# Splitting the first store of a row softmax into a 16-partition DMA and a 112-partition DMA

## The chip, the cores and the metric

The kernel runs on one core of a Trainium2 chip. A core has several engines that run at once: TensorE (unused here), VectorE (DVE in the profile), ScalarE (ACT), GpSimd (POOL) and SyncE (SP). Data moves between the chip's main memory (HBM) and the on-chip memory of 128 partitions (SBUF) by DMA; sixteen DMA engines do the moving, whichever engine issues the transfer. The metric is the device time of one execution in microseconds (us), as the median of several runs. A profiled execution also has a span, from its first to its last instruction in the trace, which is a little shorter than its own time.

## The reference

The input has 16 x 1024 rows of 512 float32 values, 33.55 MB. Each row becomes a softmax with temperature 0.5:

```python
def reference(x: np.ndarray) -> np.ndarray:
    temp = 0.5
    x_scaled = x / temp
    x_max = np.max(x_scaled, axis=-1, keepdims=True)
    exp_x = np.exp(x_scaled - x_max)
    return (exp_x / np.sum(exp_x, axis=-1, keepdims=True)).astype(np.float32)
```

The output has the same size, so 67.1 MB have to cross between HBM and SBUF.

## The kernel before, in words

The 16,384 rows are cut into eight chunks of 4 MB. In a chunk each of the 128 partitions holds 16 consecutive rows (G = 16), which is one unbroken piece of 32 KB in HBM. Six buffers hold chunks (BUFS = 6); chunks 6 and 7 go into the buffers of chunks 0 and 1 and can be loaded only when those have been stored.

SyncE issues the loads (`load`, L68): chunk 0 in two DMAs, the others in one each. Of chunk 7 the last row of each partition is loaded by GpSimd (`load_last_row`, L97), after it has copied one finished sum (L90) so that it starts late. The first six chunks are issued without waiting for any buffer.

Compute goes block by block; a block is a chunk or, in chunks 0 and 7, a part of one (BLOCKS; eleven blocks in all, three of them in chunk 0). For each block VectorE takes the negated row maxima (`shift`, L77) and doubles them (L81). ScalarE computes exp(2x + bias) row by row in place, summing each row as it goes (`exponentials`, L108). VectorE inverts the sums (L125) and multiplies most rows by them (`scale_vector`, L127), and ScalarE does the remaining rows (`scale_scalar`, L138). When the last block of a chunk is scaled, ScalarE issues the chunk's store, a DMA of 4 MB (`store`, L148). So the store instruction stands in ScalarE's own stream, between exponentials.

The order on each engine is written out by hand in the loop at the end of the kernel: the exponentials of block i+1 go ahead of the scaling of block i, the maxima of block i+2 follow, then the store of block i. Blocks 0, 1 and 2 are chunk 0, so the first store comes in the round of block 2; two exponentials of block 3 (chunk 1) are held back in that round and stand right behind the store (`rows`, with its cut of 2 for chunk 1).

`finished` collects the names of all loads, of all stores but the last chunk's, and of a few last instructions; a no-operation on SyncE at the end depends on them all. The DMA queues are named q1 (loads from SyncE), q10 (stores from ScalarE) and q0 (the two loads from GpSimd) in the profile.

Of the kernel before, what the change touches and what calls it, by code (L numbers as in the profile page):

```python
# [1 line left out]

# [4 lines left out]


@with_exitstack
def kernel(  # L10
    ctx: ExitStack,
    tc: tile.TileContext,
    x: bass.AP,
    out: bass.AP,
):
    nc = tc.nc
    fp32 = mybir.dt.float32
    P = nc.NUM_PARTITIONS
    AX = mybir.AxisListType.X
    EXP = mybir.ActivationFunctionType.Exp  # L20
    COPY = mybir.ActivationFunctionType.Copy
    MAX = mybir.AluOpType.max

    D = x.shape[-1]
    xf = x.flatten_outer_dims()
    of = out.flatten_outer_dims()
    N = xf.shape[0]

    G = 16
    C = N // (P * G)
    assert C * P * G == N
    xr = xf.rearrange("(c p g) d -> c p g d", p=P, g=G)
    outr = of.rearrange("(c p g) d -> c p g d", p=P, g=G)
    WHOLE = [(0, G)]
    LOADS = [[(0, 4), (4, G)]] + [WHOLE] * 6 + [[(0, G - 1)]]
    BLOCKS = [[(0, 4), (4, 8), (8, G)]] + [WHOLE] * 6 + [[(0, 8), (8, G)]]
    STORES = [WHOLE] * 8  # L40
    BMAX = 16
    BUFS = 6

    data = ctx.enter_context(tc.tile_pool(name="data", bufs=BUFS))
    stats = ctx.enter_context(tc.tile_pool(name="stats", bufs=6))

    ctx.enter_context(tc.manual_schedule())


    warm = stats.tile([P, 1], fp32, name="warm", bufs=1)  # L50
    nc.vector.memset(warm, 0.0)  # L51
    nc.scalar.activation(out=warm, in_=warm, func=EXP)  # L52

    chunks = {}
    blocks = [(c, lo, hi) for c in range(C) for lo, hi in BLOCKS[c]]
    n = len(blocks)
    biases, sums, recips = {}, {}, {}

    finished = []

    def load(c):
        if c < BUFS:
            chunks[c] = data.tile([P, G, D], fp32, name="xt")
        else:
            chunks[c] = chunks[c - BUFS]
        xt = chunks[c]
        for lo, hi in LOADS[c]:
            part = nc.sync.dma_start(out=xt[:, lo:hi, :], in_=xr[c][:, lo:hi, :])  # L68
            finished.append(part.ins.name)

    def shift(i):
        c, lo, hi = blocks[i]
        if c not in chunks:
            load(c)
        b = hi - lo
        negmax = stats.tile([P, BMAX], fp32, name="negmax")
        nc.vector.tensor_reduce(  # L77
            negmax[:, 0:b], chunks[c][:, lo:hi, :], axis=AX, op=MAX, negate=True
        )
        biases[i] = stats.tile([P, BMAX], fp32, name="bias")  # L80
        nc.vector.tensor_scalar_mul(biases[i][:, 0:b], negmax[:, 0:b], 2.0)  # L81

    def load_last_row(signal):
        seen = stats.tile([P, 1], fp32, name="seen", bufs=1)
        copied = nc.gpsimd.tensor_copy(out=seen, in_=signal)  # L90
        finished.append(copied.ins.name)
        c = C - 1
        halves = "p (h d) -> p h d"
        to = chunks[c - BUFS][:, G - 1, :].rearrange(halves, h=2)
        of_ = xr[c][:, G - 1, :].rearrange(halves, h=2)
        for p0, p1 in ((P - 2, P), (0, P - 2)):
            part = nc.gpsimd.dma_start(  # L97
                out=to[p0:p1], in_=of_[p0:p1], max_dma_last_dim=2 * D
            )
            finished.append(part.ins.name)  # L100

    def exponentials(i, rows):
        c, lo, hi = blocks[i]
        if i not in sums:
            sums[i] = stats.tile([P, BMAX], fp32, name="sums")
        for g in rows:
            row = chunks[c][:, lo + g, :]
            nc.scalar.activation(  # L108
                out=row,
                in_=row,  # L110
                func=EXP,
                bias=biases[i][:, g : g + 1],
                scale=2.0,
                accum_out=sums[i][:, g : g + 1],
            )
            if c == BUFS - 1 and g == 10:
                load_last_row(sums[i][:, g : g + 1])


    def scale_vector(i):  # L120
        c, lo, hi = blocks[i]
        b = hi - lo
        k = b - b // 8
        recips[i] = stats.tile([P, BMAX], fp32, name="recip")
        nc.vector.reciprocal(recips[i][:, 0:b], sums[i][:, 0:b])  # L125
        rows = chunks[c][:, lo : lo + k, :]
        last = nc.vector.tensor_mul(  # L127
            rows, rows, recips[i][:, 0:k].unsqueeze(2).broadcast_to((P, k, D))
        )
        if i == n - 1:  # L130
            finished.append(last.ins.name)

    def scale_scalar(i):
        c, lo, hi = blocks[i]
        b = hi - lo
        for g in range(b - b // 8, b):
            row = chunks[c][:, lo + g, :]
            last = nc.scalar.activation(  # L138
                out=row, in_=row, func=COPY, scale=recips[i][:, g : g + 1]
            )  # L140
            if i == n - 1:
                finished.append(last.ins.name)

    def store(i):
        c, _, end = blocks[i]
        for lo, hi in STORES[c]:
            if hi == end:
                part = nc.scalar.dma_start(  # L148
                    out=outr[c][:, lo:hi, :], in_=chunks[c][:, lo:hi, :]
                )  # L150
                if c < C - 1:
                    finished.append(part.ins.name)

    shift(0)
    shift(1)

    def rows(i):
        c, lo, hi = blocks[i]
        cut = hi - lo - (2 if c == 1 else 0)
        return range(cut), range(cut, hi - lo)  # L160

    exponentials(0, rows(0)[0])
    for i in range(n):
        if i + 1 < n:
            exponentials(i + 1, rows(i + 1)[0])
        scale_vector(i)
        scale_scalar(i)
        if i + 2 < n:
            shift(i + 2)
        store(i)  # L170
        if i + 1 < n:
            exponentials(i + 1, rows(i + 1)[1])

    seen = nc.sync.nop()
    info = mybir.DependencyInfo(
        mybir.DependencyClass.Sync, mybir.DependencyReason.DATA
    )
    for name in finished:
        tc.add_manual_dep(seen.ins, name, info, reason="leaves one wait for the end")


# [1 line left out]
_INS = ['x']  # L183
_OUTS = [((16, 1024, 512), 'float32')]


# [23 lines left out]
```

## Time and profile before

| what | value |
|---|---|
| median of three runs | 161.78 us (161.74 to 161.98) |
| the profiled execution's own time | 162.29 us |
| its span | 160.5 us |
| VectorE busy | 134.6 us, 84% |
| ScalarE busy | 102.2 us, 64% |
| GpSimd busy | 1.9 us, 1% |
| bytes moved by DMA | 67.13 MB, mean 418 GB/s over the span |
| a store (4 MB), issue to landing | 23.1 us in the median |
| a full load (4 MB), issue to landing | 34.8 us in the median |

Busy time is the sum of an engine's instructions; issuing a DMA is not counted in it. "Issue to landing" counts from the issuing instruction to the completion, so it includes time in which the transfer stood in the queue behind others or shared the DMA engines with them. In the profile's row of slices the span is cut into 40 equal parts, a digit being the busy share in tenths, and a row below gives the GB/s moved in each slice. L numbers are lines of the kernel.

### The profile page before, as it was taken

The page shows a single profiled execution, that of the slowest core. Times are in us where ns is not written, and L with a number is a line of the kernel's source. Part 1 is how long each engine was busy: PE and PEld are TensorE (multiplying, and loading weights), DVE is VectorE, ACT ScalarE, POOL GpSimd, SP SyncE. Part 2 cuts the span into 40 slices and gives each one's busy share as a digit, 9 for nine tenths or more (in the row PEclk, how much of TensorE's full clock was granted, in tenths as well). Part 3 has the DMA queues.
Part 4 walks back from the last instruction along what each step waited for, and adds up shares of the span by engine and source line. Part 5 has one row for each costly group of instructions (what it writes and reads, how often), then busy time and mean ns, then how long its engine had stood idle before and what let it go on. Part 6 is the DMA issues. An engine that isn't in the chain of part 4 may idle for free.

```text
span 160.5 us, 411 instructions
## 1 busy us (share of the span) xinstructions
DVE 134.6 (84%) x45; ACT 102.2 (64%) x273; POOL 1.9 (1%) x7
## 2 busy tenths in 40 slices
DVE  0607999999999999999999999999999999957000
ACT  3071549069989963998199909991899891790000
POOL 0000000000000000000000000030000000000000
DMA  5999999999989999999999999989999999999994
GB/s 184 470 408 498 400 392 457 457 392 402 506 269 425 490 392 400 506 400 392 490 425 392 474 434 392 490 383 483 422 450 400 400 465 441 392 457 449 400 441 204
DMA packets 2578, 67.13 MB, mean 418 GB/s; under 512 B 328, under 2 KB 328, under 8 KB 400
## 3 DMA queue, kind: packets, MB, share of 16 engines
q1 hardware_dynamic: 1296, 33.29, 49.3%
q10 hardware_dynamic: 1152, 33.55, 48.4%
q0 software_dynamic: 128, 0.26, 0.4%
q14 instruction: 2, 0.02, 0.0%
HBM read 33.55 MB, written 33.55 MB: 418 GB/s over the span
## 4 chain that ended last, share of the span: by engine, by line
DVE 75%; DMA 7%; issue 5%; ACT 3%; SPq 0%
DVE negmax L77 42%; DVE xt L127 31%; DMA xt<-in_x_dram 7%; ACT xt L108 3%; DVE bias L81 1%; DVE recip L125 1%; SPq L68 0%
## 5 line engine op out<-in xcount | busy, mean ns | idle before, releaser
L108 ACT ACTIVATE xt<-xt,bias 128x512 f32<-128x512 f32 x128 | 90.4, 708 | 41.5 <-DVE bias L81 40.6
L77 DVE TENSOR_REDUCE negmax<-xt 128x16 f32<-128x8192 f32 (+2 forms) x11 | 69.9, 6352 | 9.4 <-DMA xt<-in_x_dram 9.4
L127 DVE TENSOR_TENSOR xt<-xt,recip 128x7168 f32<-128x7168 f32 (+2 forms) x11 | 62.0, 5637 | 0.4
L108 ACT ACTIVATION_READ_ACCUMULATOR xt<-xt,bias 128x1 f32 x128 | 23.9, 187 | 0.0
L138 ACT ACTIVATE xt<-xt,recip 128x512 f32<-128x512 f32 x15 | 9.9, 706 | 0.0
L125 DVE RECIPROCAL recip<-sums 128x16 f32<-128x16 f32 (+2 forms) x11 | 2.4, 218 | 1.8 <-ACT xt L108 1.8
L81 DVE TENSOR_SCALAR bias<-negmax 128x16 f32<-128x16 f32 (+2 forms) x11 | 1.9, 173 | 0.4
L52 ACT ACT_TABLE_LOAD x1 | 1.3, 1283 | 0.7 <-PEq L194 0.7
L97 POOL DMA_DIRECT2D xt<-in_x_dram x2 | 1.5, 741 | 0.5 <-issue 0.5
L90 POOL COPY seen<-sums 128x1 f32<-128x1 f32 x1 | 0.2, 184 | 103.6 <-ACT xt L108 103.6
L51 DVE MEMSET warm<- 128x1 f32 x1 | 0.1, 59 | 0.8 <-PEq L194 0.8
L52 ACT ACTIVATE warm<-warm 128x1 f32<-128x1 f32 x1 | 0.2, 202 | 0.0
L194 POOL MEMSET const-float32-0.0<- 128x1 f32 x1 | 0.1, 93 | 0.2 <-issue 0.2
L194 POOL MEMSET const-bfloat16-1.0<- 128x1 bf16 x1 | 0.1, 95 | 0.0
L194 POOL MEMSET const-uint8-127<- 128x1 uint8 x1 | 0.1, 95 | 0.0
L194 POOL MEMSET const-float32-1.0<- 128x1 f32 x1 | 0.1, 93 | 0.0
## 6 DMA issues: line engine op xcount, KB each, us to landing
out_dram<-xt ACTq DMA_DIRECT2D x8, 4096.0 KB, 23.1
xt<-in_x_dram SPq DMA_DIRECT2D x6, 4096.0 KB, 34.8
xt<-in_x_dram SPq DMA_DIRECT2D x1, 3840.0 KB, 27.8
xt<-in_x_dram SPq DMA_DIRECT2D x1, 3072.0 KB, 11.6
xt<-in_x_dram SPq DMA_DIRECT2D x1, 1024.0 KB, 4.8
xt<-in_x_dram POOLq DMA_DIRECT2D x1, 252.0 KB, 15.4
xt<-in_x_dram POOLq DMA_DIRECT2D x1, 4.0 KB, 9.1
```

The lines of the kernel that those rows point to most:

```text
L51: nc.vector.memset(warm, 0.0)
L52: nc.scalar.activation(out=warm, in_=warm, func=EXP)
L77: nc.vector.tensor_reduce(negmax[:, 0:b], chunks[c][:, lo:hi, :], axis=AX, op=MAX, negate=True)
L81: nc.vector.tensor_scalar_mul(biases[i][:, 0:b], negmax[:, 0:b], 2.0)
L90: copied = nc.gpsimd.tensor_copy(out=seen, in_=signal)
L97: part = nc.gpsimd.dma_start(out=to[p0:p1], in_=of_[p0:p1], max_dma_last_dim=2 * D)
L108: nc.scalar.activation(out=row, in_=row, func=EXP, bias=biases[i][:, g : g + 1], scale=2.0, accum_out=sums[i][:, g : g + 1],)
L125: nc.vector.reciprocal(recips[i][:, 0:b], sums[i][:, 0:b])
L127: last = nc.vector.tensor_mul(rows, rows, recips[i][:, 0:k].unsqueeze(2).broadcast_to((P, k, D)))
L138: last = nc.scalar.activation(out=row, in_=row, func=COPY, scale=recips[i][:, g : g + 1])
L194: nc = _bacc.Bacc("TRN2", target_bir_lowering=False, num_devices=1)
```

## The change

The store of chunk 0 becomes two DMAs from the same instruction stream, one after the other: the first stores partitions 0 to 15, the second partitions 16 to 127. Sixteen partitions are sixteen pieces of 32 KB; the other DMA has 112 pieces. The stores of chunks 1 to 7 stay single DMAs of 128 partitions. Both new DMAs enter the list `finished`, and the load of chunk 6, which takes chunk 0's buffer, depends on both. The order of all other instructions on every engine is the same as before; ScalarE's stream has one instruction more.

```diff
     STORES = [WHOLE] * 8
+
+    SPLIT = [(0, 16), (16, P)]
     BMAX = 16
...
         for lo, hi in STORES[c]:
             if hi == end:
-                part = nc.scalar.dma_start(
-                    out=outr[c][:, lo:hi, :], in_=chunks[c][:, lo:hi, :]
-                )
-                if c < C - 1:
-                    finished.append(part.ins.name)
+                for p, q in SPLIT if c == 0 else [(0, P)]:
+                    part = nc.scalar.dma_start(
+                        out=outr[c][p:q, lo:hi, :], in_=chunks[c][p:q, lo:hi, :]
+                    )
+                    if c < C - 1:
+                        finished.append(part.ins.name)
```

## The prediction

> **What bounds the kernel now.** I read the slices first, to see which resource is full from end to end, then the DMA queues, to turn that into a sum, then the waits and the timeline around the first store and the last.
>
> ```profile
> DVE  0607999999999999999999999999999999957000
> ACT  3071549069989963998199909991899891790000
> ...
> DMA  5999999999989999999999999989999999999994
> GB/s 184 470 408 498 400 392 457 457 392 402 506 269 425 490 392 400 506 400 392 490 425 392 474 434 392 490 383 483 422 450 400 400 465 441 392 457 449 400 441 204
> ```
>
> The DMA engines are full from the first slice to the last, also after VectorE and ScalarE have stopped. One slice of about 4 us falls out: 44 to 48 us at 269 GB/s, where the first store is issued.
>
> ```profile
> q1 hardware_dynamic: 1296, 33.29, 49.3%
> q10 hardware_dynamic: 1152, 33.55, 48.4%
> q0 software_dynamic: 128, 0.26, 0.4%
> ```
>
> Loads are q1, stores q10, the last row's loads q0; together 98.1% of 16 engines. The 1152 packets of q10 are eight stores of 128 pieces (one partition, 32 KB) and 16 completions. 48.4% of 160.5 us is 77.7 us per engine for 64 pieces: 1.21 us a piece, 27 GB/s per engine. No compute stage can be shortened to any use here; a microsecond in which an engine moves nothing is a microsecond at the end.
>
> ```profile
> SPq L68 <- DMA out_dram<-xt: 74.7, 2, 55.8
> DVE negmax L77 <- DMA xt<-in_x_dram: 9.4, 2, 4.8
> 43.36 0.71 ACT L138 ACTIVATE xt<-xt,recip 128x512 f32<-128x512 f32 x1
> 44.10 0.37 ACTq L148 DMA_DIRECT2D out_dram<-xt  x1
> 44.52 0.72 ACT L108 ACTIVATE xt<-xt,bias 128x512 f32<-128x512 f32 x1 [0.45 <-ACT xt L138]
> 46.31 0.72 ACT L108 ACTIVATE xt<-xt,bias 128x512 f32<-128x512 f32 x1 [0.27 <-DVE bias L81]
> 147.48 0.34 ACTq L148 DMA_DIRECT2D out_dram<-xt  x1
> ```
>
> The first two are waits (total, times, longest), the rest the timeline: VectorE waits for loads only at the start (twice), SyncE's two last loads wait for stores 0 and 1, and the first and last stores go out at 44.10 and 147.48 us. The chain of waits names VectorE for 75% of the span, but it ends with the last multiply at 147.4 us and leaves out the store behind it: it is not what sets the end.
>
> The trace's records of single DMA packets give the sum (their clock stands about 10.1 us ahead of the span). The first data packet starts at 2.0 us, the last ends at 159.45, and 1.05 us follow. At the usual duration of each size the packets of an engine make 155.55 us; they took 157.49, so 1.93 us are stretched packets: 0.53 in the first 2 us, 0.3 scattered, and **1.08 us per engine in 18 load packets between 45 and 49 us**, which took 1.36 to 2.49 us in place of 1.21. They begin before any store packet moves (the first at 48.66 us). No such stretch stands where later stores, or later loads, are queued behind running ones. So the first store costs about 1.1 us at its start, once.
>
> [...] from 50 us on store and load packets of 1.21 us alternate. [...]
>
> **The change part by part.** It removes one issue of a 4 MB store and adds two, of 0.5 and 3.5 MB; bytes and pieces are the same, the other seven stores are untouched.
>
> *ScalarE's queue.* One more issue of 0.34 to 0.37 us at 44.5 us. Behind it stand two exponentials of block 3 (44.52 and 45.24) and block 4's. ScalarE was idle for 0.27 us at 46.31, so block 4 starts about 0.1 us late; the next gap, 4.0 us before 62.93, swallows that, and VectorE wants these sums only at 62.80, when the last was done at 57.7. Without that cover it would cost 0.37 us. Cost: 0.
>
> *Completions.* q10 gets 16 more packets (1168), one of 9 ns per engine: 0.01 us. Since that packet takes one turn of the store queue, the loads move one piece ahead: no byte more.
>
> *Waits.* Load 6 waits for two DMAs in place of one. Store 0 lands at 68.5 us by the packets, the load queue has work until 75.3 to 76.8: at least 6.8 us of cover. The closing wait gets one more name that is long done: 0.
>
> *The start of the first store (1.08 us today).* Not resolved by the trace. If it is a fixed price of waking the store queue, nothing changes: 0. If it lasts while the descriptors of that DMA are written, a first DMA with an eighth of them pays an eighth: 1.08 x 7/8 = 0.94 us gained, 1.08 at most. I take 0 here, since the stretch was about one piece long (1.21 us) and one piece each is still what comes first.
>
> *The 16-partition piece.* Sixteen engines each read 32 KB from partitions 0 to 15. [...] In the trace three engines took their first store piece about 1.2 us before the other thirteen, so their reads would be almost over; [...] **2.7 us**. I take this.
>
> *The 112-partition piece.* [...] Load turns fall between them[...], so I take 0 in the forecast and 2.1 at the upper end.
>
> Sum: 0 + 0.01 + 0 + 0 + 2.7 = +2.7 us on a saturated stream, 1:1 at the end. The profiled execution took 162.29 us with a span of 160.5, so 1.8 us lie outside, unchanged; its new span would be 163.2. It stands 0.5 us above the median of the runs, 161.78; I put the difference on the median: **164.5 us**.
>
> **The rivals.**
>
> *The wake-up stretch shrinks[...]: faster.* For it: the dip is the one clear hole in the stream, at just this store, and stores queued behind a running one show none. Against it: that a shorter first DMA shortens it rests on the descriptor reading alone. Time: 161.78 - 0.94 = 160.85. [...] There is room at the end: the last store is issued at 147.5 us and the engines finish the one before between 148.7 and 149.8, so 1.2 us can be gained before compute limits.
>
> *Nothing moves.* The stretch is a fixed price, and [...] waiting engines move loads. Time: 161.8.
>
> [...] 2.7 + 2.1: 166.6. [...]
>
> **How the numbers follow.** A measurement of this kernel tells about 0.2% (0.32 us) from nothing. Contention: 0.50, of which 0.15 at 0.4 to 1.5 us (reads partly hidden), 0.22 around 2.7, 0.13 from 3.5 to 4.8. Faster: 0.29, between 160.7 and 161.4. Nothing: 0.21. So the time is that of the middle contention case, 164.5; the range from 160.8 to 166.0 leaves out the very end on both sides, about 0.05 below and 0.07 above. The likeliest case alone is 162.3 to 166.6.
>
> **What would show it.** Right: q10 at 1168 packets with a share of 50% or more in place of 48.4%; store packets of partitions 0 to 15 of 2 to 5 us just after 48 us; a slice of 48 to 52 us well below 400 GB/s; the first store landing 2 to 3 us later, the multiplies and exponentials at the same durations, and the last packet near 162 us. If all 32 KB store packets stay at 1.21 us, [...] the sum of the load stretch near 46 to 49 us tells whether the change gains (near 0.1 us left) or does nothing (1.1 us again). A stretch that grows with the second DMA, or a load queue running dry before load 6, would be a loss that I have not counted.

## The result and the profile after

The changed kernel takes 167.53 us in the median of six runs (165.31 to 167.74), against 161.78 us before: 5.75 us more, a ratio of 1.0321 with a 95% interval of 1.0265 to 1.0377. The direction was forecast; the size was not, and 167.53 lies outside the range of 160.8 to 166.0. The runs also scatter over 2.4 us, where those of the kernel before lie within 0.24 us.

The profiled execution took 167.55 us with a span of 165.5 us. The rows of slices of the changed kernel, DMA share and GB/s, and its DMA queues (packets, MB, share of 16 engines):

```profile
DMA  5998999989898999999999999999999999999950
GB/s 194 440 507 380 475 412 404 483 380 493 388 380 356 380 428 404 428 428 412 459 404 444 412 432 430 412 453 399 432 462 444 388 475 404 459 428 436 444 222 16
...
q10 hardware_dynamic: 1168, 33.56, 48.2%
q1 hardware_dynamic: 1296, 33.29, 47.3%
```

The 16 extra completions are there, of 9 ns each; of the 16 between 51 and 54 us, 12 stand between two load packets. The store queue's share did not rise to the 50% that was named as a sign; the forecast's own sum, 77.7 + 2.7 us of a span of 163.2, would have given 49.3%. A slice is now 4.14 us long, so shares have to be turned into time: stores 48.2% of 165.5 us, 79.8 us per engine against 77.7 before; loads 78.3 us against 79.1. Together that is only 1.2 us more. The rest of the 5 us is at the right end: the last two slices move 222 and 16 GB/s. Most engines have stopped there, and a few work on. The windows (length, busy time of DVE, ACT and POOL with instructions, TensorE clock, DMA share, GB/s) show it, first of the changed kernel:

```profile
44.00:48.00 4.00, 3.66 (x4) 3.09 (x9) 0.00 (x0) 1.00 0.97 393
48.00:52.00 4.00, 4.00 (x1) 4.00 (x13) 0.00 (x0) 1.00 0.97 279
...
159.00:162.00 3.00, 0.00 (x0) 0.00 (x0) 0.00 (x0) 1.00 0.33 142
162.00:165.50 3.50, 0.00 (x0) 0.00 (x0) 0.00 (x0) 1.00 0.02 9
```

and of the kernel before:

```profile
44.00:48.00 4.00, 3.93 (x4) 3.28 (x10) 0.00 (x0) 1.00 0.93 287
48.00:52.00 4.00, 4.00 (x1) 4.00 (x13) 0.00 (x0) 1.00 0.91 393
...
156.00:159.00 3.00, 0.00 (x0) 0.00 (x0) 0.00 (x0) 1.00 0.79 339
159.00:160.50 1.50, 0.00 (x0) 0.00 (x0) 0.00 (x0) 1.00 0.00 0
```

Before, all engines stop within about a microsecond. After, a 2% share (about a third of one engine, on average over the window) remains from 162 us on: one engine that is late. The slow stretch near the first store has moved from 44 to 48 us into 48 to 52 us, out of the loads and into the store's own pieces.

The records of single DMA packets give the numbers behind this. Packets were put on their engines by the rule that each starts as the one before it ends; that makes sixteen chains, with small slips, and their ends are sure (sixteen packets are under way at once for 147 us in both runs, 17 to 19 for 8.6 us).

| per engine, us | before | after |
|---|---|---|
| load packets stretched at 44 to 49 us, mean | 1.08 | 0.22 |
| first store's sixteen pieces, above 1.21 each, mean (range) | 0 | 1.30 (0.51 to 2.81) |
| other store packets, 52 to 70 us, above 1.21, mean | 0 | 0.69 |
| last packet of an engine: mean over engines | 159.14 | 160.50 |
| last packet of the first engine to stop | 158.40 | 158.62 |
| last packet of the last engine | 159.45 | 164.56 |

The last engine to stop had store packets of 4.02 us at 48.7, 3.53 us at 56.4 and 2.16 us at 68.5 us. Its chain still holds 64 store pieces, the same as the mean engine's, and the ends lie 5.94 us apart, nearly five pieces: nothing that it lost was taken over by another. The mean engine lost 1.4 us; the time went up by what the unluckiest lost, 5.1 us.

ScalarE's part of the timeline after:

```profile
44.00 0.85 ACTq L151 DMA_DIRECT2D out_dram<-xt  x2
44.91 0.72 ACT L110 ACTIVATE xt<-xt,bias 128x512 f32<-128x512 f32 x1 [0.93 <-ACT xt L140]
...
46.46 0.25 DVE L127 RECIPROCAL recip<-sums 128x16 f32<-128x16 f32 x1 [0.27 <-ACT xt L110]
46.75 7.63 DVE L129 TENSOR_TENSOR xt<-xt,recip 128x7168 f32<-128x7168 f32 x1
...
147.76 0.34 ACTq L151 DMA_DIRECT2D out_dram<-xt  x1
```

Two issues take 0.85 us in place of 0.37. The two exponentials behind them end late, and VectorE, which wants their sums at once for block 3, waits 0.27 us. That delay runs through to the last store (147.76 against 147.48 us), which still waits for engines that are busy until 148.9 us and later.

The load of chunk 6 was touched as well. Store 0 landed at 74.3 us in place of 68.5, so this load was issued at 74.4 us, and its first packets moved at about 78.7 us; thirteen of the sixteen engines had done their last packet of load 5 before 76 us, the first at 73.9. So the load queue stood empty for 3 to 5 us on most engines. They moved stores meanwhile: per engine, packets were busy for 1.32 us more than before, and the mean end moved by 1.36, which leaves no room for idle engines.

### The profile page after: what moved, and what is told of

Same layout as the page of the kernel before. It is cut to its first block, busy times and chain, and to the rows that moved or that the text cites. A ratio compares the mean times of both kernels' runs of the same rounds, so it can differ in the third digit from the quotient of the medians.

```text
span 165.5 us, 413 instructions
## 1 busy us (share of the span) xinstructions
DVE 134.7 (81%) x45; ACT 102.1 (62%) x273; POOL 1.9 (1%) x7
## 3 DMA queue, kind: packets, MB, share of 16 engines
q10 hardware_dynamic: 1168, 33.56, 48.2%
## 4 chain that ended last, share of the span: by engine, by line
DVE 65%; ACT 10%; DMA 7%; issue 6%; ACTq 0%; SPq 0%
DVE negmax L79 35%; DVE xt L129 28%; ACT xt L110 9%; DMA xt<-in_x_dram 7%; DVE recip L127 1%; DVE bias L83 1%; ACTq L151 0%; ACT xt L140 0%; SPq L70 0%
```

## The experiments

The theory on trial, T: in a DMA that takes only part of the 128 partitions, the engines at work at the same time slow each other down when those partitions lie close together in SBUF; the loss is what the unluckiest engine collects. (A trace does not say which partition a packet reads, nor what engines would share; T can be tried only by what the packets' durations do when the partitions are chosen differently.) Where an expectation has a figure for T, it stands first; the factors of four and two in such figures were the author's estimate. Rivals: R1, the loss comes from neighbouring addresses in HBM, not from SBUF; R2, it belongs to the beginning of the store queue, or to one DMA more; and for the stretch of 1.08 us in the kernel before, three guesses: the number of pieces in the first DMA (the prediction's descriptors), a piece read ahead, the first use of a queue.

### Where the split stands: at chunk 1, and at chunk 5

```diff
-                for p, q in SPLIT if c == 0 else [(0, P)]:
+                for p, q in SPLIT if c == 1 else [(0, P)]:
```

> The split is made at chunk 1 in place of chunk 0, where the store queue is already running beside the loads. [...] stretched store packets again when these pieces are moved, at about 68 to 90 us, and 165 to 168 us; the stretch at 46 us is back at 1.08 us. If the loss belongs to the first use of the store queue or to its first store, the time is near 161.8 us.

Measured: 167.20 us (166.62 to 168.13), ratio 1.033 (1.029 to 1.037), the same loss as at chunk 0. The stretch of loads at 44 to 49 us is back at 0.88 us, and the stretched store packets are now at 68 to 86 us, the first sixteen costing 1.49 us in the mean. The first half of R2 falls: the store queue had been running for 20 us. One DMA more is there in this kernel too; that half is settled further below, where the 112 pieces alone, with no DMA more, stretch store packets, and a split with one DMA more, but with all partitions in each, stretches no packet of its store.

With `c == 5` the split stands where no load runs any more.

> The 16 and 112 split, made at chunk 5 in place of chunk 0, in the stretch where only stores run. [...] the sixteen pieces take 4.85 us each, 3.6 us more than 1.21; of the 112, [...] up to 2.1 us more per engine. In all 3.6 to 6 us above 161.8, [...] 165.4 to 168 us. [...]

Measured: 173.12 us (172.71 to 174.20), ratio 1.071 (1.066 to 1.076): 11.3 us more, about twice the upper end of what was expected (3.6 to 6). A window of it, from the arrival of the sixteen pieces on, and one of the pieces behind them:

```profile
129.00:134.00 5.00, 5.00 (x2) 4.89 (x14) 0.00 (x0) 1.00 1.07 229
134.00:150.00 16.00, 11.44 (x6) 6.98 (x18) 0.00 (x0) 1.00 0.99 348
```

The first sixteen took up to 5.73 us, most of them 2.9 to 3.3 us: 2.5 us above 1.21 in the mean, where 3.6 was expected. The 112, put at 2.1 us at most, were stretched by 3.1 us per engine in the mean until 150 us, and engines ended between 161.7 and 170.1 us. The mean end moved by 5.2 us, inside what was expected; the last engine's by 10.7 us. So the mean was about right (the sixteen cost less than expected, the 112 more), and the spread was left out. That the 112 cost more here than beside loads fits T, since beside loads about every second packet is a load's (before, 52 to 66 us: 107 store packets and 99 of the load queue); this is a reading and was not tried by itself.

### SBUF or HBM: four stores of chunk 5 by sixteen partitions at a time

Four kernels store chunk 5 by eight DMAs of 16 partitions. The partitions are neighbours or lie 8 apart in SBUF; the blocks of 32 KB that they go to are neighbours or lie 8 apart in HBM. Where these differ, chunk 5 is loaded by the same pairs, so that each row still lands where it belongs.

The store of the second of them:

```diff
+                parts = (
+                    [(chunks[c][j:P:8], outr[c][16 * j : 16 * j + 16]) for j in range(8)]
+                    if c == 5
+                    else [(chunks[c], outr[c])]
+                )
+                for sb, hbm in parts:
+                    part = nc.scalar.dma_start(out=hbm[:, lo:hi, :], in_=sb[:, lo:hi, :])
```

In the others the slices `j:P:8` and `16 * j : 16 * j + 16` are put on the sides that their names say.

Neighbours in both:

> The split is taken away from chunk 0; chunk 5 is stored by eight DMAs of 16 neighbouring partitions, at a time when only stores run. [...] each of the 128 store packets takes up to 4.85 us (4 x 1.21) and the store 38.8 us in place of 9.7: about 29 us more. If neighbouring pieces are no matter, 1.21 us each and 161.8 us.

SBUF 8 apart, HBM neighbours:

> Chunk 5 is loaded and stored by eight DMAs of 16 partitions that lie 8 apart, each against the same 16 neighbouring blocks of HBM as in the kernel with sixteen neighbours. [...] each store packet takes 2.43 us, the store 19.4 us. If neighbouring addresses in HBM are the cause, the packets are as long as with sixteen neighbours (4.85 us). The load of chunk 5 is split in the same way and will lose time too, so only the store packets after 125 us tell, not the total.

SBUF neighbours, HBM 8 apart:

> Chunk 5 is loaded and stored by eight DMAs of 16 neighbouring partitions, each against 16 blocks of HBM that lie 8 blocks (256 KB) apart. [...] as with sixteen neighbours on both sides: store packets up to 4.3 to 4.7 us and about 23 us for the chunk. HBM: a store like that of partitions 8 apart or better, packets near 2.5 us or less. The load of chunk 5 is split too, so only the store packets after 125 us tell, not the total.

8 apart in both:

> Chunk 5 is loaded as before and stored by eight DMAs of 16 partitions that lie 8 apart, each against its own blocks of HBM, 256 KB apart. [...] 2.4 to 2.6 us a packet as in the kernel that had neighbouring HBM blocks, about 20 us for the chunk and some 10 us on the total, 172 us. If the distance in HBM matters, the packets differ from 2.5 us.

| SBUF, HBM | time, us | store packets of chunk 5 above 1.3 us: median, longest, us | the chunk took, us |
|---|---|---|---|
| near, near | 177.14 | 2.95, 4.65 | 23 |
| 8 apart, near | 186.45 | 2.52, 2.83 | 20 |
| near, 8 apart | 206.77 | 3.05, 5.06 | 26 |
| 8 apart, 8 apart | 172.91 | 2.48, 2.78 | 18 |

The second and third totals contain the split load of chunk 5 and are not to be compared. The packets are: their length follows the distance in SBUF, whatever the distance in HBM, so R1 falls. The fourth total is the one that was expected (172). In the third kernel the engines were idle before this store and took its first pieces in step, which is the cleanest case; its window, and then one of the second kernel (SBUF 8 apart):

```profile
154.00:159.00 5.00, 5.00 (x1) 0.00 (x0) 0.00 (x0) 1.00 0.98 105
```

```profile
141.00:151.00 10.00, 10.00 (x2) 0.00 (x0) 0.00 (x0) 1.00 1.02 210
```

Sixteen neighbours in step: 105 GB/s, the sixteen packets 4.90 us in the mean, 4.04 times 1.213. Sixteen that lie 8 apart: 210 GB/s, packets of about twice 1.21 us (2.52 in the median). What the engines share was not shown; the factors of four and two were. The miss is the first kernel: 15 us more, not 29. Its packets are as long as 4.65 us, but taken together its engines move twice what the sixteen in step moved in the third kernel (105 GB/s):

```profile
129.00:139.00 10.00, 8.39 (x3) 0.00 (x0) 0.00 (x0) 1.00 1.05 203
```

My reading, which was not tried by itself, is that engines that get ahead go on to the next DMA's sixteen partitions and leave the others more room. So the factor of four is shown for the sixteen of the third kernel that began in step (4.90 us), and not for these packets, with 2.95 us in the median.

### The two DMAs, each without the other

```diff
-    SPLIT = [(0, 16), (16, P)]
+    SPLIT = [(16, P)]
```

> The DMA of partitions 0 to 15 is left out (these rows of chunk 0 are not stored); that of 112 stays. 1.21 us less work per engine. [...] one or a few engines collect 2 to 4 us of stretched packets and the time is 162 to 164 us; if the loss was the sixteen pieces alone, no store packet is stretched and the time falls to what compute sets, about 161 us.

Measured: 163.98 us (162.99 to 164.62), ratio 1.011 (1.008 to 1.014), with 1.21 us less for each engine to move. Its slices:

```profile
DMA  5999899999899999999999999999999999999980
GB/s 181 464 435 468 387 468 435 395 500 397 387 387 387 443 387 411 403 427 443 427 427 443 435 423 421 442 429 426 433 442 427 452 411 427 452 427 411 411 387 24
```

No dip near the store stands out, and still the last slice moves 24 GB/s. Half the engines end by 158.51 us, but the last two at 160.24 and 161.64. Without any stretch the last would end at 159.45 - 1.21 = 158.24. So the 112 pieces alone cost the slowest engine about 3.4 us, while store packets are stretched by 0.9 us per engine in the mean.

The other way round, with `SPLIT = [(0, 16)]`:

> The DMA of partitions 16 to 127 is left out (these rows of chunk 0 are not stored); that of 16 partitions stays. 8.5 us less work per engine, so the engines run dry before the last store and the total is set by compute and that store, about 161 us: it tells little. The packets tell: if the sixteen pieces cost what they cost in the changed kernel, each is stretched by 0.5 to 2.8 us at about 48 to 53 us, 1.3 us in the mean, and no store packet later is. If the sixteen pieces were stretched by the 112 behind them, they take 1.21 us here.

Measured: 161.54 us, which says little, as expected. Fifteen of the sixteen pieces take 1.61 to 2.88 us at 48 to 52 us (1.02 us above 1.21 in the mean), and no other store packet at that stage is stretched. The sixteen pieces by themselves cost an engine 1.7 us at most here, where they cost up to 2.81 with the 112 behind them (one profile of each).

### The other order

```diff
-    SPLIT = [(0, 16), (16, P)]
+    SPLIT = [(16, P), (0, 16)]
```

> The DMA of 112 partitions goes first, then the one of 16. [...] 164 to 168 us and single engines that end several us after the others. Stretch before the first store: with the descriptor reading about 7/8 of 1.08 us, 0.95; if it is the read-ahead of one piece, then near 1 us[...].

Measured: 165.65 us (165.50 to 166.08), ratio 1.024 (1.021 to 1.026). The sixteen pieces, last, still take up to 4.21 us, and engines end between 159.3 and 162.5 us. As T has it. The stretch of loads is 0.89 us, which fits both readings.

### The stretch at the first store

Can the 1.08 us be had without a cut across the partitions? A split by rows keeps all 128 in each DMA:

```diff
+                for g0, g1 in [(0, 1), (1, G)] if c == 0 else [(lo, hi)]:
+                    part = nc.scalar.dma_start(
+                        out=outr[c][:, g0:g1, :], in_=chunks[c][:, g0:g1, :]
+                    )
```

> Chunk 0 is stored by two DMAs of all 128 partitions each: row 0 (pieces of 2 KB), then rows 1 to 15 (30 KB). [...] no store packet should be stretched. If the stretch of load packets before the first store (1.08 us per engine before) is one piece that the engine reads ahead, it shrinks to about 0.1 us and the time is about 160.8 us. If it is the time in which the descriptors of the first DMA are written (128 of them, as before), it stays at 1.1 us and the time at 161.8 us.

Measured: 163.29 us (163.20 to 163.77), ratio 1.009 (1.007 to 1.011): slower, which neither reading gave. The windows of this kernel:

```profile
44.00:50.00 6.00, 5.93 (x4) 5.36 (x15) 0.00 (x0) 1.00 0.99 425
50.00:54.00 4.00, 4.00 (x2) 4.00 (x13) 0.00 (x0) 1.00 1.01 358
```

The packets of this store are at their usual 84 ns and 1.14 us, as T says of DMAs with all partitions. From 44 to 50 us the 2 KB pieces go out and no load is stretched, though both DMAs had been issued by 44.3 us, each of 128 pieces: the guess by their number falls. The stretch comes at 51 to 56 us (0.84 us), around the first 30 KB pieces (54.6 us), as it came before the first 32 KB piece (48.66 us) in the kernel before. A large piece read ahead would fit that place, though not the small total that was expected from it. The small pieces have a price of their own: the 2 KB pieces (84 ns) go out between load pieces of 32 KB (1.21 us), so loads run ahead, store 0 lands only at 71.8 us (68.5 before), and the load queue, whose last piece landed at 70.7 us, stands empty until 76 us, when load 6 comes. A second stretch of loads, 0.98 us, follows at 84 to 87 us; what causes it is not known.

Two kernels use ScalarE's queue earlier. One loads the first 4 rows of chunk 0 through it:

```diff
+            queue = nc.scalar if c == 0 and lo == 0 else nc.sync
+            part = queue.dma_start(out=xt[:, lo:hi, :], in_=xr[c][:, lo:hi, :])
```

> As the kernel before, but the first load (4 rows of chunk 0) is issued from ScalarE's queue, so that this queue has been used once, at the start. If the stretch of 1.08 us at the first store is a price of the first use of the queue, it is gone and the time is about 160.7 us. If it comes each time the store queue begins beside running loads, it stays and the time is 161.8 us, 0.3 us more if the start is later.

Measured: 165.79 us (165.67 to 166.20), ratio 1.024 (1.022 to 1.026). The stretch at the first store is nearly gone (0.11 us), but the load, now beside the 3 MB behind it, lands 13.8 us after its issue (4.8 before):

```profile
DVE negmax L78 <- DMA xt<-in_x_dram: 13.8, 1, 13.8
```

VectorE starts at 14.7 us in place of 5.5, the last store goes out at 152.5 us (147.5 before), and compute sets the end. Load packets are stretched by 0.69 us at 84 to 87 us here too.

The other sends one small load through that queue first:

```diff
+    early = stats.tile([P, 128], fp32, name="early", bufs=1)
+    touched = nc.scalar.dma_start(out=early, in_=xr[0][:, 0, 0:128])
```

> As the kernel before, with one small load (512 bytes for each partition, into a tile that nobody reads) issued first on ScalarE's queue. It costs about 0.15 us of the DMA engines at the start. If the stretch of 1.08 us at the first store is a price of the first use of this queue, it goes and the time is about 160.9 us; if not, it stays and the time is 161.9 us.

Measured: 162.62 us (162.28 to 162.85), ratio 1.005 (1.003 to 1.006). The stretch at 46 to 52 us is 0.68 us in the mean in place of 1.08, and the engines' median end is 158.69 us, 0.5 us earlier than before; but one load packet took 2.73 us, the last engine ended at 160.13, and the kernel is slower. The cause of the stretch stays open: the number of pieces in the first DMA alone does not explain it, it isn't only the first use of the queue, and a read-ahead of one piece does not explain the stretches at 84 to 87 us. It is also not a fixed 1.08 us: in the eight other kernels whose first store has 128 or 112 partitions and pieces of 32 KB, with the queue not used earlier, it is 0.74 to 0.89 us; in the two that begin with sixteen pieces it is 0.22 and 0.25.

No version here that stores every row beats the kernel before.

## Why the prediction was wrong

*What bounds the kernel* held: compute was 0.3 us later and it cost nothing, and every loss came from the DMA engines. The completions (1168 packets) held as well. *The wait of load 6* cost nothing, but not for the reason given: of the cover of 6.8 us nothing was left, since store 0 landed 5.8 us later. The load queue ran dry on most engines, which the prediction named as a loss not counted; stores filled the gap.

*ScalarE's queue* was costed at 0 with a wrong cover. The second issue cost 0.48 us, and VectorE was not free of it: the two exponentials behind the store belong to block 3, whose sums VectorE wants at 46.2 us, not at 62.8. It waited 0.27 us. The full DMA queue hid this, not the gap that was named.

*The start of the first store*, 1.08 us, was kept at 0 change. It fell to 0.22 us. The gain of 0.86 is close to the 0.94 us of the rival with the smaller first DMA, but not for its reason: the split by rows, with as many pieces in its first DMA as the whole store, had no stretch while these pieces moved. In the changed kernel the sixteen pieces that follow lose 1.30 us, more than the 0.86 that the loads no longer do.

*The sixteen pieces* were put at 2.7 us, the author's estimate, read from no trace; they cost 1.30 us in the mean and 2.81 at most. That sixteen neighbours slow each other down was right: 4.90 us a packet where they were in step, in the third of the four stores of chunk 5. As a mean the size was twice too large: in the changed kernel the sixteen began within 0.77 us (48.47 to 49.24) and took 1.72 to 4.02 us. On the engine that ended last the piece cost 2.81 us, near the 2.7 by chance: the 2.7 was not about that engine.

*The 112 pieces* are the step that failed. "I take 0 in the forecast and 2.1 at the upper end." The mean is small indeed, 0.69 us, but the end is not set by the mean. The stretched packets pile up on single engines: the engine that ended last lost 3.35 us to them (2.31, 0.09 and 0.95), and without the sixteen pieces they made the slowest about 3.4 us late. How often pieces of the 112 hinder each other, from which the 2.1 came, was the author's estimate and was not shown; that they alone stretch store packets was (0.9 us per engine).

*The sum* carried that error: it added what an engine loses on average to a time that is set by the last of sixteen. With means it would have been 0.01 - 0.86 + 1.30 + 0.69 = 1.1 us, near the 1.36 us by which the mean end moved; the last engine's end moved by 5.11. Where 2.7 + 0 was forecast, that engine lost 2.81 + 3.35. The rival that charged both DMAs, 2.7 + 2.1, 166.6 us, was the nearest, and is still 0.9 us short. Its bounds were worked out for an average engine, and so the upper end of the range was too low.

*"Nothing moves" and "faster"* fell: the sixteen pieces do go to one engine each (all were under way from 49.24 to 50.23 us), and they are not free: they took 1.72 us and more in place of 1.21.

## What to carry to other kernels

In a kernel that is full of DMA from end to end, as this one is, a transfer is best left with all 128 partitions in each DMA: so all 1024 store pieces of the kernel before took 1.21 to 1.26 us. A cut along the rows stretched no packet of its store either (84 ns and 1.14 us), but with its 2 KB pieces it cost 1.4 us too, so it is no free cut either. The cut across partitions cost most where only stores ran (11.3 us, against 5.4 and 5.7 beside loads). And because no engine here took over what another had lost, what such a change costs is to be read from the engine that stops last, not from the mean share or GB/s.

## What was not expected of the hardware

- Engines that move neighbouring partitions at once are not slowed alike: of the sixteen neighbours in the stage with stores alone, four took 5.29 to 5.73 us and most of the others 2.9 to 3.3 us.
- The loss differs between executions by up to 2.4 us, for a reason that was not shown; the kernel with whole stores stayed within 0.24 to 0.69 us in each of its five sets of runs.
- In the split by rows, pieces of 2 KB (84 ns) went out between load pieces of 32 KB (1.21 us), and the load queue ran ahead: loads landed at 70.7 us in place of 76.8.
- When the store queue begins beside full loads, load packets can be stretched once by 0.2 to 1.1 us per engine; two of the kernels show 0.7 to 1.0 us of this again at 84 to 87 us, some 8 us after their load queue had begun anew.
